# Four kinds of subtraction and addition in the projection sweeps move from GpSimd to VectorE

## The chip, the cores and the metric

The kernel runs on one core of a Trainium2 chip. The metric is the device time of one execution in microseconds. Three executions of the kernel before took 2745.77, 2746.82 and 2751.03 us; the median is 2746.82 us. TensorE (PE) multiplies matrices; VectorE (DVE), ScalarE (ACT) and GpSimd (POOL) do elementwise work; SyncE (SP) issues most transfers. Each engine works through its own list of instructions in a fixed order and waits on semaphores for the others.

## The reference

One layer of a hybrid decoder, for a prompt of 2048 tokens and 64 new tokens (8 sequences of 8), with model width 1024:

```python
xn   = rmsnorm(x, g_pre_mix)
proj = xn @ w_in                      # q_a k_a v_a | q_b k_b v_b r_b | a_lr
o_a  = attn_fn(q_a, k_a, v_a)         # three dilated windows, 8 heads x 64
logf = log_sigmoid(a_lr @ w_a2 + b_a) / 16
o_b, s_new = gla_recurrent(q_b, k_b, v_b, logf, s_gla)   # 4 heads, dk 64, dv 128
o_b  = rmsnorm(o_b, g_gla_norm) * silu(r_b)
x    = x + rmsnorm(concat(o_a, o_b) @ w_o, g_post_mix)
f    = conv_ffn(rmsnorm(x, g_pre_ffn), ...)              # width 2816, gelu
x    = x + rmsnorm(f, g_post_ffn)
```

Everything is float32. `gla_recurrent` takes a running sum of `logf` within each chunk of tokens and exponentials of it; `rmsnorm` needs the sum of squares of each token over 1024 features.

## The kernel before, in words

A float32 product is made of three products in PE's faster float32 format (fp32r). Each operand is split into a high part (`hi`, a rounded copy, made on ACT) and a low part (`lo = src - hi`, one subtraction of two SBUF tensors), and PE sums `hi*hi + hi*lo + lo*hi`. `split` (L67 to L73) does this; its fourth argument names the engine of the low part, "p" for GpSimd and "v" for VectorE. L70 in the profile is the high part, L73 the low part on either engine.

The layer is computed in three stages. The **sweeps** (`sweeps`, from L257) project the normalized input, 512 tokens (576 with the new ones) at a time. The token blocks are numbered c = 0 to 3 and are passed over twice. Sweep B (c = 0, 1, 2, 3, the first 430 us or so) makes the columns of the linear attention (GLA), and the GLA recurrence itself is interleaved with it. Sweep A (c = 3, 0, 1, 2, to about 770 us) makes q, k and v of the window attention, and the attention of the new tokens is interleaved with it. Then come the window attention of the prompt and the tail (output projection and feed-forward network), which runs to the end.

What the change touches, all of it in the sweeps:

- `norm_pre` (L159) sums the squares of the next block's input over the 8 feature tiles: ACT squares a tile into `sq` (one buffer), and an addition collects it in `ssq` (L177). For c = 0 the addition stands on VectorE, for c = 1 to 3 on GpSimd.
- `xhat` (L205) scales the 8 tiles of the next block (L228, two SBUF tensors, on VectorE) and splits them into `xh` and `xl` (L238). The low parts of even tiles stand on VectorE, those of odd tiles on GpSimd. The first block of sweep B has a path of its own (L235).
- `wfill` (L373) loads the weights ahead of their use, a buffer of 512 KB at a time, and splits them into `wh` and `wl`, four buffers of each. Sweep B's 12 weights (numbers 12 and up) are split once, on VectorE, and kept in memory for later blocks; sweep A's 12 are split anew for each of the 4 blocks, with the low part on GpSimd, 48 in all.
- `gla_decay` (L609) makes the running sum of the decay for the two halves of the heads: `lfm` and `gB` on VectorE (L631, L632), an exponential and a logarithm on ACT (L633, L637), a subtraction (L640: GpSimd for c = 1 to 3), and the running sum as a scan on VectorE (L641).

Behind the scan, `gla_p` makes the decayed keys and queries (`gkh` L751, `gqt` L754 and L757, `gqh` L762, `ktb` L768), PE transposes `gkh` into `pkt` (L752), and the state of the recurrence `gS` is updated on VectorE from the PSUM tile `pgo` (copies at L837, updates at L839). The projections of sweep B end in PSUM tiles `pq` and `pv` (three banks in turn, named g1); for the gate columns ACT takes a tanh `th` of `pv` (L695) and VectorE multiplies it with `pv` (L696), which frees the bank. In sweep A VectorE copies `pv` to `vs` (L65) and makes `ql` from `pq` (L432, L73).

The order of the instructions on each engine is not the order of the code: the program is built with `schedule_with_timeline_sim=True`, and a scheduler that has its own estimate of each instruction's time decides where each one stands in its engine's list. An instruction that changes its engine therefore also moves others, on all engines.

## Time and profile before

| | before |
|---|---|
| median of three executions | 2746.82 us |
| the profiled execution | 2747.31 us |
| span of its trace, first to last instruction | 2745.3 us |
| PE busy | 2655.9 us (97%) |
| VectorE busy | 1791.5 us (65%) |
| ScalarE busy | 1270.2 us (46%) |
| GpSimd busy | 587.2 us (21%) |
| mean clock granted to PE | 0.989 |

The trace holds one execution. A row of the timeline gives the start of an instruction in us, its duration, the engine, the source line, the operation, output and inputs, shapes, a count where rows are merged, and in brackets the engine's idle time before it with what ended it. A row of a group of instructions gives the count, then busy us and mean ns of one, then the idle time before them. A row of a table of windows gives, for each stretch, its length, the busy time of PE, PE's weight loads (PEld), DVE, ACT and POOL with their instruction counts, the share of PE's clock that was granted (PEclk), the share of the transfer engines and GB/s. The time outside the span of the profiled execution is 2747.31 - 2745.3 = 2.0 us.

### The profile page before, as it was taken

The numbers are of one execution on the slowest core, as the hardware profiler recorded it, in microseconds if no ns is written. First come the engines' busy times: TensorE is split into PE (matmuls) and PEld (weight loads), VectorE is DVE, ScalarE is ACT, GpSimd is POOL, SyncE is SP. The second block draws the span as 40 slices with busy tenths as digits, with TensorE's granted clock in tenths as the row PEclk, the third lists the DMA queues.
The fourth block names the chain that finished last, engine by engine and source line by source line (L and its number), as shares of the span: only waits on it lengthen the run. The fifth ranks groups of instructions, "written<-read, shape, count | busy, mean of one in ns | idle before, by whom it ended". The sixth has DMA issues, their size and how long they took to land. (4 is left out here: it accounts for less than half of the span.)

```text
span 2745.3 us, 58213 instructions
## 1 busy us (share of the span) xinstructions
PE 2655.9 (97%) x22203; PEld 2520.9 (92%) x22203; DVE 1791.5 (65%) x4338; ACT 1270.2 (46%) x2961; POOL 587.2 (21%) x643
## 2 busy tenths in 40 slices
PE   8999999999999998998999998999999999999997
PEld 6899899888788887998999998999999999999997
DVE  7545544444357776468899889865676665766666
ACT  6535433333368784445555455433344332443332
POOL 4435243433345674012000020000110000200001
PEclk9999999999999999999999999999999999999998
DMA  8755436799776663376677588986698766976654
GB/s 316 254 182 190 165 116 218 264 334 370 267 260 193 191 168 108 127 249 258 249 274 288 196 323 299 341 303 207 239 341 289 279 227 211 327 249 216 215 192 148
DMA packets 287015, 661.67 MB, mean 241 GB/s; under 512 B 32960, under 2 KB 82752, under 8 KB 284688
## 3 DMA queue, kind: packets, MB, share of 16 engines
q1 hardware_dynamic: 256528, 579.53, 61.1%
q0 software_dynamic: 13216, 46.56, 5.1%
q10 hardware_dynamic: 16992, 31.86, 3.1%
q8 instruction: 175, 2.87, 0.4%
q14 instruction: 104, 0.85, 0.1%
HBM read 511.45 MB, written 146.37 MB: 240 GB/s over the span
## 5 line engine op out<-in xcount | busy, mean ns | idle before, releaser
L70 ACT ACTIVATE ws<-wr 128x512 fp32r<-128x512 f32 (+1 forms) x482 | 292.8, 616 | 426.2 <-PE pfe L1628 138.6
L92 PE MATMUL pfd<-hh,ws 128*128 128x264 f32 x2816 | 474.6, 285 | 6.8 <-ACT ws L70 5.6
L92 PEld LDWEIGHTS pfd<-hh,ws 128*128 128x128 f32 x2816 | 400.0, 189 | 9.2 <-ACT ws L70 7.4
L73 DVE TENSOR_TENSOR ws<-wr,ws 128x512 fp32r<-128x512 f32 (+1 forms) x482 | 319.4, 668 | 119.5 <-ACT ws L70 115.7
L92 PE MATMUL pfd<-hl,ws 128*128 128x264 f32 x1408 | 301.5, 285 | 1.8 <-DVE hl L73 1.8
L1628 PE MATMUL pfe<-xh,ws 128*128 128x264 f32 x1496 | 290.3, 286 | 12.1 <-DVE u L1615 7.6
L1628 PE MATMUL pfa<-xh,ws 128*128 128x264 f32 x1496 | 289.8, 285 | 4.5 <-ACT ws L70 1.9
L1628 PE MATMUL pfd<-xh,ws 128*128 128x264 f32 x1408 | 289.3, 285 | 2.1 <-ACT ws L70 1.0
L1628 PEld LDWEIGHTS pfe<-xh,ws 128*128 128x128 f32 x1496 | 236.5, 189 | 13.8 <-DVE u L1615 8.4
L1628 PEld LDWEIGHTS pfa<-xh,ws 128*128 128x128 f32 x1496 | 234.9, 188 | 6.0 <-ACT p L1617 2.4
L399 PE MATMUL pv<-wh,xh 128*128 128x256 f32 (+1 forms) x816 | 236.1, 289 | 1.8 <-DVE th L696 1.8
L1628 PEld LDWEIGHTS pfd<-xh,ws 128*128 128x128 f32 x1408 | 231.3, 189 | 3.1 <-ACT ws L70 1.2
L399 PE MATMUL pv<-wh,xl 128*128 128x256 f32 (+1 forms) x816 | 232.2, 285 | 0.0
L399 PE MATMUL pv<-wl,xh 128*128 128x256 f32 (+1 forms) x816 | 232.2, 285 | 0.0
L92 PEld LDWEIGHTS pfd<-hl,ws 128*128 128x128 f32 x1408 | 225.1, 189 | 2.1 <-DVE hl L73 2.0
L1577 POOL DMA_DIRECT2D xl<-d_xst x52 | 28.1, 541 | 830.8 <-PE pfe L1628 495.4
L1869 ACT ACTIVATE ass<-ass,aml 128x256 f32<-128x256 f32 (+1 forms) x384 | 173.5, 454 | 63.7 <-DVE aml L1865 37.9
L1628 PE MATMUL pfd<-xl,ws 128*128 128x264 f32 x704 | 200.6, 285 | 0.7 <-DMA xl<-d_xst 0.7
L92 PE MATMUL pq<-xh,wh 128*128 128x512 f32 (+2 forms) x480 | 170.9, 364 | 10.7 <-ACT xh L234 7.9
L1628 PE MATMUL pfe<-xl,ws 128*128 128x264 f32 x616 | 175.7, 285 | 0.0
L1628 PE MATMUL pfa<-xl,ws 128*128 128x264 f32 x616 | 174.8, 284 | 0.0
L92 PE MATMUL pq<-xl,wh 128*128 128x512 f32 (+2 forms) x480 | 174.0, 364 | 0.0
(335 smaller groups left out, 6531.6 us busy)
## 6 DMA issues: line engine op xcount, KB each, us to landing
ws<-d_wst SPq DMA_DIRECT2D x248, 512.0 KB, 5.2
wr<-in_wu SPq DMA_DIRECT2D x114, 512.0 KB, 5.0
d_wst<-ws SPq DMA_DIRECT2D x88, 512.0 KB, 4.1
wr<-in_wd SPq DMA_DIRECT2D x160, 256.0 KB, 3.8
wr<-in_wt SPq DMA_DIRECT2D x60, 512.0 KB, 7.0
wh<-d_wbs SPq DMA_DIRECT2D x35, 512.0 KB, 5.6
wl<-d_wbs SPq DMA_DIRECT2D x35, 512.0 KB, 5.8
skp<-in_ckt SPq DMA_DIRECT2D x16, 1024.0 KB, 8.1
```

Source lines behind the costliest of these rows:

```text
L70: h = nc.scalar.activation(hi, src, AF.Copy)
L73: return h, (nc.gpsimd if lo_eng == "p" else nc.vector).tensor_tensor(lo, src, hi.bitcast(F32), op=ALU.subtract)
L92: mm = nc.tensor.matmul(o, ww[:, k, :], xx[:, s0:s0 + n], start=(k == order[0] and i == 0), stop=(k == order[-1] and i == 2))
L399: mm = nc.tensor.matmul(ps[:m, :256], x[:, t0:t0 + m], w[:, k % 4, :], start=(k == 0 and i == 0), stop=(k == KT - 1 and i == 2))
L1577: self.nc.gpsimd.dma_start(t.bitcast(F32), xo[i, z])
L1628: self.lastmm = nc.tensor.matmul(bank[:, :H], w[:, ww, k, :], xx, start=new and k == 0 and j == 0, stop=k == 3 and j == 2, skip_group_chec ...
L1869: ex = nc.scalar.activation(ssb[:, sc:sc + nk], ssb[:, sc:sc + nk], AF.Exp, bias=self.ml[:, idx, h:h + 1], scale=-1.0, accum_out=self.ml[: ...
```

## The change

Four conditions that chose GpSimd are taken out, and VectorE does the work in every case. GpSimd keeps the other GLA multiplications (L701, L757, L762, L768) and the small power functions (L107).

```diff
@@ norm_pre
                 nc.scalar.activation(sq[:, :w], r[:, :w], AF.Square)
-                (nc.gpsimd if c else nc.vector).tensor_tensor(ssq[:, :w], ssq[:, :w], sq[:, :w], op=ALU.add)
+                nc.vector.tensor_tensor(ssq[:, :w], ssq[:, :w], sq[:, :w], op=ALU.add)
@@ xhat
             else:
-                self.split(hi[:, :w], lo[:, :w], r[:, :w], "p" if k % 2 else "v")
+                self.split(hi[:, :w], lo[:, :w], r[:, :w], "v")
@@ wfill
-                w = self.weight(self.a["wt"][i].rearrange("p (k c) -> p k c", k=nk), sh, "v" if i >= 12 else "p")
+                w = self.weight(self.a["wt"][i].rearrange("p (k c) -> p k c", k=nk), sh, "v")
@@ gla_decay
         for i, (m, B) in enumerate(zip(ms, self.gB)):
-            (nc.gpsimd if c else nc.vector).tensor_tensor(m[:, :w], m[:, :w], B[:, :w], op=ALU.subtract)
+            nc.vector.tensor_tensor(m[:, :w], m[:, :w], B[:, :w], op=ALU.subtract)
```

103 instructions leave GpSimd's list and join VectorE's: 48 `wl`, 28 `xl`, 21 `ssq` and 6 `lfm`. The scheduler then sets all lists anew. Three places matter below.

**PE in sweep B, block c = 0**, around the first transpose of the decayed keys (`pkt` from `gkh`). The numbers tell the buffers apart: `pv_603` is the fourth projection block of 128 tokens, `pv_658` the fifth, each of 24 matmuls. Before:

```order
L399 MATMUL pv_603<-wh_404,xl_198 128x256
L399 MATMUL pv_603<-wh_404,xh_206 128x256
L399 MATMUL pv_603<-wl_405,xh_206 128x256
L752 MATMUL pkt_560<-c_ident,gkh_561 128x128
L399 MATMUL pv_603<-wh_404,xl_207 128x256
L399 MATMUL pv_603<-wh_404,xh_210 128x256
```

After:

```order
L399 MATMUL pv_658<-wh_455,xl_198 128x256
L399 MATMUL pv_658<-wh_455,xh_206 128x256
L752 MATMUL pkt_560<-c_ident,gkh_561 128x128
L399 MATMUL pv_658<-wl_456,xh_206 128x256
L399 MATMUL pv_658<-wh_455,xl_207 128x256
L399 MATMUL pv_658<-wh_455,xh_210 128x256
```

The transpose now stands 23 matmuls later in PE's list.

**VectorE at the start of sweep B's block c = 1**, where the decay's scan and the state's copies stand (`gB_1361` and `lfm_1362` are the first half of the heads, `gB_1368` and `lfm_1369` the second). Before:

```order
L641 SCALAR_TENSOR_TENSOR gB_1361<-smask,lfm_1362 128x512
L646 TENSOR_SCALAR gbt_1378<-gB_1361 128x4x4
L647 TENSOR_SCALAR gbt_1378<-gB_1361 128x4
L754 TENSOR_TENSOR gqt_1776<-gB_1361 128x128
L768 TENSOR_TENSOR ktb_128<-ktb_128,gk_1421 128x32
L837 COPY gS_117<-pgo_1479 64x128 x2
L751 TENSOR_TENSOR gkh_1772<-gkh_1772,gk_1421 128x128
L768 TENSOR_TENSOR ktb_128<-ktb_128,gk_1421 128x96
L641 SCALAR_TENSOR_TENSOR gB_1368<-smask,lfm_1369 128x512
L839 SCALAR_TENSOR_TENSOR gS_115<-gS_117,gEc_557,pgo_1506 64x128 x2
```

After:

```order
L640 TENSOR_TENSOR lfm_1362<-lfm_1362,gB_1361 128x512
L641 SCALAR_TENSOR_TENSOR gB_1361<-smask,lfm_1362 128x512
L177 TENSOR_TENSOR ssq_1730<-ssq_1730,sq_2103 128x512
L646 TENSOR_SCALAR gbt_1378<-gB_1361 128x4x4
L647 TENSOR_SCALAR gbt_1378<-gB_1361 128x4
L640 TENSOR_TENSOR lfm_1369<-lfm_1369,gB_1368 128x512
L754 TENSOR_TENSOR gqt_1776<-gB_1361 128x128
L837 COPY gS_117<-pgo_1479 64x128 x2
L641 SCALAR_TENSOR_TENSOR gB_1368<-smask,lfm_1369 128x512
L177 TENSOR_TENSOR ssq_1730<-ssq_1730,sq_2108 128x512
L768 TENSOR_TENSOR ktb_128<-ktb_128,gk_1421 128x32
L839 SCALAR_TENSOR_TENSOR gS_115<-gS_117,gEc_557,pgo_1506 64x128 x2
```

The first copy of the state moves ahead of `ktb`; two additions of `ssq`, each of which waits for a square on ACT, now stand in front of `gbt` and of the state's update at L839.

**VectorE where sweep B passes into sweep A** (`wl_4851` and `wl_5158` are the first two weights of sweep A). Before:

```order
L65 COPY vb_4117<-pv_4792 128x256
L65 COPY gkT_4764<-pkt_4723 128x256
L65 COPY vb_4118<-pv_4818 64x256
L65 COPY vb_4114<-pv_4854 128x256
L65 COPY vb_4115<-pv_4892 128x256
```

After:

```order
L65 COPY vb_4117<-pv_4792 128x256
L65 COPY gkT_4764<-pkt_4723 128x256
L73 TENSOR_TENSOR wl_4851<-wr_4848,wh_4850 128x1024
L65 COPY vb_4118<-pv_4818 64x256
L73 TENSOR_TENSOR wl_5158<-wr_5155,wh_5157 128x1024
L65 COPY vb_4114<-pv_4854 128x256
L65 COPY vb_4115<-pv_4892 128x256
```

The low parts of the weights, which wait for `wh` on ACT, now stand between the copies that empty PSUM banks.

## The prediction

> **What bounds the kernel now.** I read the table of windows first, cut at the ends of sweep B, sweep A and the window attention.

> ```profile
> 0.00:430.00 430.00, 403.80 (x3307) 363.23 (x3308) 239.06 (x581) 215.24 (x567) 182.94 (x238) 0.98 0.61 210
> 430.00:770.00 340.00, 339.48 (x2868) 285.27 (x2867) 135.45 (x289) 110.50 (x169) 132.89 (x76) 1.00 0.81 290
> ```

> PE bounds both sweeps. In sweep A it is idle for 0.5 of 340 us: nothing can be won there. In sweep B it is idle for 26.2 of 430 us. The change can pay only through that idle time, so I read next what ended it, in the table of PE's waits up to 760 us (total, times, longest).

> ```profile
> PE pq L92 <- ACT xh L234: 7.9, 1, 7.9
> PE pgo L843 <- DVE gS L839: 5.0, 2, 4.1
> PE pkt L752 <- DVE gkh L751: 2.3, 1, 2.3
> PE pq L92 <- DVE ql L432: 2.3, 1, 2.3
> PE pgo L830 <- DVE gS L837: 1.9, 1, 1.9
> PE pv L399 <- DVE th L696: 1.8, 1, 1.8
> PE pgo L830 <- DVE gS L839: 1.8, 2, 0.9
> ```

> The first row is the wait for the first input at the start; the change does not touch it. The other six add up to 15.1 us, and VectorE ends every one of them. VectorE is both what the change loads and what PE waits for.

> Some of these waits cost more than their own length. The windows just behind three of them:

> ```profile
> 50.30:53.70 3.40, 3.19 (x15) 3.22 (x16) 3.40 (x9) 3.40 (x14) 3.12 (x5) 0.50 0.43 143
> 57.10:60.60 3.50, 3.50 (x19) 3.50 (x18) 3.26 (x10) 2.80 (x7) 3.27 (x6) 0.51 0.50 170
> 323.40:330.20 6.80, 5.84 (x23) 5.48 (x24) 5.07 (x19) 5.37 (x25) 4.08 (x10) 0.50 0.00 1
> ```

> The granted clock is half there. 13.7 us at half clock are worth up to 6.8 us of PE's work. Idle time and half clock together, 15.1 + 6.8 = 21.9 us, are about all that could be won.

> **What VectorE pays now for GpSimd's work.** The timeline of GpSimd (two rows) and VectorE at the start of sweep A:

> ```profile
> 402.33 2.90 POOL L73 TENSOR_TENSOR wl<-wr,wh 128x1024 fp32r<-128x1024 f32 x1
> 405.19 3.86 POOL L73 TENSOR_TENSOR xl<-raw,xh 128x576 fp32r<-128x576 f32 x2
> ```

> ```profile
> 400.39 2.59 DVE L73 TENSOR_TENSOR xl<-raw,xh 128x576 fp32r<-128x576 f32 x1
> 403.76 2.08 DVE L228 SCALAR_TENSOR_TENSOR raw<-raw,c_gvec,rbp 128x576 f32<-128x576 f32 x1
> 405.77 2.00 DVE L73 TENSOR_TENSOR xl<-raw,xh 128x576 fp32r<-128x576 f32 x1
> 407.69 1.91 DVE L228 SCALAR_TENSOR_TENSOR raw<-raw,c_gvec,rbp 128x512 f32<-128x512 f32 x1
> 410.30 0.69 DVE L73 TENSOR_TENSOR xl<-raw,xh 128x512 fp32r<-128x512 f32 x1 [0.70 <-ACT xh L70]
> 410.90 0.75 DVE L228 SCALAR_TENSOR_TENSOR raw<-raw,c_gvec,rbp 128x512 f32<-128x512 f32 x1
> ```

> The same scaling takes 1.91 us beside GpSimd's `xl` and 0.75 us without it. While GpSimd runs one of its long two-input operations, a two-input operation of VectorE stands still. So the moved work leaves one engine and also ends part of another's delay.

> **The load.** Prices per instruction, from the groups up to 770 us (the fifth from the groups behind it, where GpSimd is nearly idle):

> ```profile
> L73 POOL TENSOR_TENSOR wl<-wr,wh 128x1024 fp32r<-128x1024 f32 x48 | 119.5, 2496 | 156.6 <-ACT wh L70 135.2 <-DMA out_o_vp<-vs 14.1 <-PE pgo L942 6.9
> L73 DVE TENSOR_TENSOR wl<-wr,wh 128x1024 fp32r<-128x1024 f32 x12 | 15.1, 1257 | 3.0 <-ACT wh L70 3.0
> L70 ACT ACTIVATE wh<-wr 128x1024 fp32r<-128x1024 f32 x60 | 63.4, 1056 | 104.6 <-PE pq L92 45.4 <-PE pv L399 28.6 <-issue 14.1
> L177 DVE TENSOR_TENSOR ssq<-ssq,sq 128x512 f32<-128x512 f32 x7 | 4.8, 687 | 0.1
> L73 DVE TENSOR_TENSOR ws<-wr,ws 128x512 fp32r<-128x512 f32 x450 | 306.3, 686 | 109.9 <-ACT ws L70 106.1 <-DMA wr<-in_wu 1.1 <-DMA out_o_y<-acc 0.2
> L73 DVE TENSOR_TENSOR xl<-raw,xh 128x512 fp32r<-128x512 f32 x20 | 24.3, 1220 | 3.1 <-ACT xh L70 3.0
> ```

> VectorE gets 48 x 1.257 = 60.3 us of `wl`; 28 `xl`, 21 `ssq` and 6 `lfm` at 0.69 us each (those of 576 columns by 576/512 more) make another 39 us. That is some 99 us on 374.5 us busy in 770 us. It gets back part of the delays: the 20 `xl` it already makes take 1220 ns where 686 are needed, 10.7 us in that group alone. VectorE would be busy for about 60% of the sweeps. It does not become the bound by its sum; what counts is the places where PE waits.

> **Place A, sweep B's first block (48 to 61 us).**

> ```profile
> 50.51 0.45 PE L752 MATMUL pkt<-c_ident,gkh 128*128 128x128 f32 x1 [2.30 <-DVE gkh L751]
> 50.41 1.40 ACT L767 ACTIVATE ktb<-gB,gbt 128x128 f32<-128x128 f32 x5
> 53.20 1.29 POOL L177 TENSOR_TENSOR ssq<-ssq,sq 128x512 f32<-128x512 f32 x1
> 53.27 2.29 DVE L754 TENSOR_TENSOR gqt<-gB 128x128 f32<-128x128 f32 x3
> 55.95 0.39 PE L399 MATMUL pv<-wh,xh 128*128 128x256 f32 x1 [1.81 <-DVE th L696]
> 46.80 0.28 PE L399 MATMUL pv<-wh,xh 128*128 128x256 f32 x1
> 46.91 0.28 PE L399 MATMUL pv<-wl,xh 128*128 128x256 f32 x1
> ```

> By the new order the transpose stands 23 matmuls later, 23 x 0.11 = 2.5 us: that covers the 2.30 us unless `gkh` is later than now. ACT's new list has one `sq`, one `th` and a table load in front of `gkh`, so I expect about 1 us of lateness, no more. The `th` that PE waits for at 55.95 stood behind three `gqt`, held up by the addition on GpSimd; it now stands ahead of them. The next `th` then sets the pace: ACT has ten of the small exponentials, at 1.40/5 = 0.28 us each, between `gkh` at about 51 us and that `th`, which with VectorE's part comes to about 54.4 us. PE starts the sixth block there, where now it starts the fifth at 55.95, one block of 24 x 0.11 = 2.6 us less far. 55.95 + 2.6 - 54.4 = 4.2 us, and 0.3 for the half clock behind it that goes: **-4.5 us**, between 0 (the wait only moves) and -7.5 (4.1 of waits and 3.4 of half clock).

> [...]

> **Place B, the start of block c = 1 (120 to 140 us).**

> ```profile
> 123.28 1.28 ACT L760 ACT_TABLE_LOAD   x1
> 125.12 0.33 DVE L768 TENSOR_TENSOR ktb<-ktb,gk 128x32 f32<-128x32 f32 x1 [2.19 <-ACT ktb L767]
> 126.04 0.48 PE L830 MATMUL pgo<-vb,gkT 128*128 128x256 f32 x1 [1.86 <-DVE gS L837]
> ```

> VectorE stood idle for 2.19 us here: ACT set the time, through table loads, not GpSimd. The copy of the state now stands ahead of `ktb`, but behind an `ssq` and the second `lfm`, both of which wait for ACT. By the list it can start at about 124.6 instead of 125.38: **-0.8 us**, between +3 (the added `ssq` hold it) and -2.8 (its share of the six rows). Block c = 2 has two waits of 0.9 us behind the same kind of work, with less of ACT in them: **-0.8**, between 0 and -1.8.

> **Place C, block c = 3.**

> ```profile
> 315.12 2.80 POOL L640 TENSOR_TENSOR lfm<-lfm,gB 128x576 f32<-128x576 f32 x2 [11.05 <-ACT gB L637]
> 316.57 2.43 DVE L641 TENSOR_TENSOR_SCAN gB<-smask,lfm 128x512 f32<-128x512 f32 x1 [3.50 <-POOL lfm L640]
> 319.44 1.21 DVE L641 TENSOR_TENSOR_SCAN gB<-smask,lfm 128x512 f32<-128x512 f32 x1
> 324.36 0.79 PE L843 MATMUL pgo<-gS,gqh 128*128 128x256 f32 x1 [4.12 <-DVE gS L839]
> ```

> The scan beside the second `lfm` takes 2.43 instead of 1.21 us: 1.2 us come back. The two `lfm` at 0.75 on VectorE end the wait for GpSimd 1.4 us sooner and then fill the same 1.5 us. In front of the second state update nothing else goes. The wait shrinks to about 2.9 us, and a little of the 3.4 us that the half clock costs: **-1.5**, between +1 and -7.5.

> **Place D, into sweep A (413 us).** PE waited 2.3 us for `ql`, behind the stretched rows shown above. The four stretched rows from 400 us on lost 5.5 us against 0.77 us for 576 columns and 0.69 to 0.75 for 512; two `wl` (2.5 us) and three `xl` (2.3 us) take their place: 5.5 - 4.8, **-0.7**, between +2 and -2.3.

> **Sweep A.** A `wl` on VectorE waits for `wh`, and `wh` for a buffer that PE gives back; behind it in VectorE's list stand the copies that empty PE's banks. On GpSimd 135.2 us of such waiting harmed nobody. The cover is the banks: three in turn, so a copy may be 2 x 2.6 us late before PE stops. A `wh` and its `wl` (1.06 + 1.26 us) fit into that. I put **+0.5 us**, between 0 and +8 (48 of them at 0.17).

> **The sum**: -4.5 - 0.8 - 0.8 - 1.5 - 0.7 + 0.5 = -7.8 us. The profiled execution took 2747.3 us (span 2745.3 and 2.0 around it), so 2739.5; it lies 0.5 above the median shown, so 2739.0.

> **Rivals.**
> - *Only the contention goes, and it was not on the path* (within 0.2%). ACT's one list with its table loads sets places A and B, as the 2.19 us row says. Then only C and D give anything, 2.2 us: 2744.6. Against it: at 55.95 and 316.57 GpSimd's own rows stretch VectorE's.
> - *All of PE's waits go, half clock with them.* 2746.8 - 21.9 = 2725. For it: the stretch is in most of these places. Against: the change adds instructions to the same list.
> - *VectorE's list becomes the wait* (slower). At the starts of the blocks c = 1 to 3 the seven `ssq` each wait for a square on ACT, and `gbt`, scan and state stand behind them. If each of three blocks lost 4 us (seven additions at 0.69 less what was idle) and the half clock followed for 3.4 us each (1.7 lost), it is 3 x 5.7 = +17, less the 5.2 us of A and D: 2759. It decides from 5.2/3 = 1.7 us a block on. For it: rows at 125.12 and 126.04 show the state held up by a neighbour that waits for ACT. Against: VectorE is idle for 191 of 430 us in sweep B.
> - *The weights' low parts hold the banks in sweep A* (slower): 48 x 0.35 us = +17, less the 8.3 us of the other terms: 2755. The 0.5 us of idle time in that sweep now speaks against.

> [...]

> **How the numbers follow.** Forecast 0.50; waits all gone 0.12; not on the path 0.22; VectorE's list 0.11; sweep A's banks 0.05. The range for 8 in 10 is 2727 to 2751: from near the second rival to half of the way to the slower ones; the forecast's own is 2731 to 2741, from twice the sum to the bound of 0.2%. A measurement of this kernel tells 0.2% (5.5 us) from no change. Faster 0.50 + 0.12 = 0.62, same 0.22, slower 0.16.

> **What would show it.** Right: no GpSimd `wl`, `xl` or `ssq`; the scaling at L228 and `xl` near 0.75 and 0.69 us everywhere in the sweeps; PE's waits before 430 us down from 15.1 to 7 to 10 us; the transpose at about 51 us without the half clock; sweep A still without idle PE. Wrong: a wait of more than 4 us at a block's start with `ssq` in front of what PE waits for, or PE idle in sweep A behind `wl`. If the time moves while PE's waits up to 770 us do not, the cause is in the stages behind, which I hold unchanged.

## The result and the profile after

The change makes the kernel faster by about 0.4%.

| | before | after |
|---|---|---|
| median of 20 executions, us | 2747.06 | 2737.48 |
| lowest and highest, us | 2740.91, 2755.08 | 2732.78, 2744.36 |
| ratio, 95% interval | | 0.9964, 0.9955 to 0.9972 |
| span of the profiled execution, us | 2745.3 | 2737.9 |

The medians are 9.6 us apart; 7.8 us were forecast. One execution of one kernel differs from the next by several us, so a place of the program that differs by 1 us between two traces proves nothing by itself.

The table of windows of the kernel after, cut as before:

```profile
0.00:430.00 430.00, 411.90 (x3345) 366.63 (x3346) 262.96 (x643) 218.27 (x578) 104.59 (x188) 1.00 0.61 214
430.00:770.00 340.00, 338.73 (x2868) 284.44 (x2866) 173.52 (x363) 114.11 (x181) 17.32 (x30) 1.00 0.81 292
```

PE is idle for 18.1 us of the first 430, where it was 26.2. In sweep A it is idle for 1.3 of 340 us. VectorE is busy for 436.5 us up to 770, 62 us more than before, although some 99 us of work went to it: the stretching ended. These are its groups up to 770 us:

```profile
L73 DVE TENSOR_TENSOR wl<-wr,wh 128x1024 fp32r<-128x1024 f32 x60 | 73.5, 1225 | 44.7 <-ACT wh L70 37.0 <-DMA raw<-in_xp 6.5 <-ACT qh L431 1.1
L73 DVE TENSOR_TENSOR xl<-raw,xh 128x512 fp32r<-128x512 f32 x40 | 26.8, 684 | 8.3 <-ACT xh L70 8.2
L228 DVE SCALAR_TENSOR_TENSOR raw<-raw,c_gvec,rbp 128x512 f32<-128x512 f32 x24 | 17.7, 751 | 4.9 <-DMA raw<-in_xp 4.5 <-ACT rbp L212 0.3
L641 DVE TENSOR_TENSOR_SCAN gB<-smask,lfm 128x512 f32<-128x512 f32 x8 | 9.8, 1221 | 0.1
```

`xl` took 1220 ns and takes 684; the scaling at L228 took 1104 ns and takes 751. The rows that VectorE ends in the table of PE's waits up to 760 us (total, times, longest; a row of 0.4 us is left out):

```profile
PE pgo L830 <- DVE gS L839: 3.6, 3, 1.9
PE pv L399 <- DVE th L696: 2.2, 3, 1.0
PE pgo L846 <- DVE gS L837: 1.2, 1, 1.2
PE pkt L752 <- DVE gkh L751: 1.1, 2, 0.6
PE pgo L843 <- DVE gS L839: 0.5, 2, 0.3
PE pq L92 <- DVE ql L432: 0.4, 1, 0.4
```

These six rows add up to 9.0 us, where the prediction's six made 15.1; not all name the same pair. With the small rows that both lists leave out it is 9.4 us after 17.5. The half clock in the sweeps was 13.7 us and is 3.4 us, at another place:

```profile
220.62:224.04 3.42, 1.56 (x9) 1.22 (x9) 3.37 (x12) 3.41 (x11) 0.55 (x2) 1.00 0.40 111
224.04:227.45 3.41, 3.41 (x18) 3.41 (x17) 2.43 (x6) 3.41 (x14) 1.80 (x5) 0.50 0.21 39
319.00:330.00 11.00, 10.60 (x74) 9.75 (x74) 9.52 (x36) 10.77 (x46) 6.17 (x14) 1.00 0.27 96
```

The last row is the start of block c = 3: before, PE waited 4.12 us there and ran 6.8 us at half clock; now it is idle for 0.4 of 11 us at the full clock.

### Where the time went, place by place

The projections are the same 3888 matmuls in every kernel of this study, in the same order but for neighbours that change places (119 of them in the kernel after). So the start of the n-th of them can be compared between two traces, and the change of that difference over a stretch is what the stretch won or lost. The table is worked out in this way from the profiled executions. Its columns are the predicted places; the first 44 us, which differ by up to 2.5 us from one execution to the next, are left out. PE's other matmuls lie between the projections and can cross the bound of a column. "Measured" is the difference of the medians from the same session's kernel before.

| kernel (profiled) | A, to 90 us | c = 1, to 184 | c = 2, to 277 | c = 3, to 394 | D, to 446 | sweep A | sum | measured |
|---|---|---|---|---|---|---|---|---|
| *predicted* | -4.5 | -0.8 | -0.8 | -1.5 | -0.7 | +0.5 | -7.8 | |
| the change | -2.5 | +1.2 | +3.8 | -6.7 | -2.9 | -0.8 | -7.9 | -9.6 |
| `wl` alone | -0.3 | -1.5 | +1.1 | -1.0 | -2.8 | +2.4 | -2.1 | -0.5 |
| `xl` alone | +1.1 | -0.6 | +4.6 | -2.6 | 0.0 | -2.2 | +0.3 | +1.3 |
| `ssq` alone | -3.0 | +3.8 | +1.2 | -0.8 | +0.7 | 0.0 | +1.9 | +2.9 |
| `lfm` alone | +1.0 | +2.2 | +1.7 | -5.0 | +0.6 | 0.0 | +0.4 | +1.9 |
| `xl` and `wl` | -0.1 | -0.5 | +4.5 | -5.9 | -2.8 | -0.8 | -5.7 | -7.0 |
| all but `ssq` | -1.3 | +0.2 | +3.8 | -5.8 | -2.8 | -0.8 | -6.6 | -8.7 |
| new lists, old engines | -1.7 | +2.4 | +4.0 | -5.3 | -1.8 | -0.8 | -3.1 | -4.9 |
| old lists, new engines | +0.9 | -1.8 | +1.6 | -5.1 | -2.2 | -0.7 | -7.3 | -9.0 |
| one input on GpSimd | -2.6 | +0.2 | +0.4 | -3.6 | -0.9 | -0.8 | -7.3 | -4.5 |
| squares late, block 3 | -2.5 | 0.0 | +2.4 | -5.6 | -2.9 | -0.8 | -9.3 | -9.7 |
| squares late, blocks 2, 3 | -3.0 | -0.5 | +2.6 | -7.0 | -2.9 | -0.8 | -11.4 | -11.3 |

The sums of the traces lie within 3 us of the measured differences. The total of the forecast holds, but hardly one of its terms does. In these columns the change takes 8.6 us from PE's idle time and 10.2 us from its time at half clock, which is worth 5.1 (in the kernel before, the 128x256 matmuls of L399 start 0.21 us apart at half clock and 0.11 at the full one). That makes 13.7 us, and only 7.9 arrive. Most of the rest goes into PE's own list, as "The loss at c = 2" shows.

### The profile page after: what moved, and what is told of

Same layout as the page of the kernel before. It is cut to its first block, busy times and chain, and to the rows that moved or that the text cites. A ratio compares the mean times of both kernels' runs of the same rounds, so it can differ in the third digit from the quotient of the medians.

```text
span 2737.9 us, 58183 instructions
## 1 busy us (share of the span) xinstructions
PE 2658.4 (97%) x22203; PEld 2518.3 (92%) x22203; DVE 1845.9 (67%) x4441; ACT 1271.2 (46%) x2961; POOL 386.4 (14%) x540
## 5 line engine op out<-in xcount | busy, mean ns | idle before, releaser
L70 ACT ACTIVATE ws<-wr 128x512 fp32r<-128x512 f32 (+1 forms) x482 | 292.9, 616 | 426.8 <-PE pfe L1628 133.6
L92 PE MATMUL pfd<-hh,ws 128*128 128x264 f32 x2816 | 476.7, 286 | 6.0 <-ACT ws L70 4.5
L92 PEld LDWEIGHTS pfd<-hh,ws 128*128 128x128 f32 x2816 | 402.1, 190 | 8.6 <-ACT ws L70 6.4
L73 DVE TENSOR_TENSOR ws<-wr,ws 128x512 fp32r<-128x512 f32 (+1 forms) x482 | 319.2, 668 | 123.7 <-ACT ws L70 118.9
L92 PE MATMUL pfd<-hl,ws 128*128 128x264 f32 x1408 | 303.1, 286 | 1.9 <-DVE hl L73 1.9
L1628 PE MATMUL pfe<-xh,ws 128*128 128x264 f32 x1496 | 291.4, 287 | 11.4 <-DVE u L1615 6.9
L399 PE MATMUL pv<-wh,xh 128*128 128x256 f32 (+1 forms) x816 | 233.9, 287 | 2.2 <-DVE th L696 2.2
L399 PE MATMUL pv<-wl,xh 128*128 128x256 f32 (+1 forms) x816 | 232.1, 284 | 0.0
L399 PE MATMUL pv<-wh,xl 128*128 128x256 f32 (+1 forms) x816 | 232.0, 284 | 0.0
L92 PEld LDWEIGHTS pfd<-hl,ws 128*128 128x128 f32 x1408 | 226.6, 190 | 2.2 <-DVE hl L73 2.1
L92 PE MATMUL pq<-xh,wh 128*128 128x512 f32 (+2 forms) x480 | 173.0, 366 | 8.3 <-ACT xh L234 7.9
L1656 DVE TENSOR_TENSOR acc<-acc,pfd 128x264 f32<-128x264 f32 x304 | 116.3, 422 | 89.6 <-PE pfd L92 89.1
L92 PE MATMUL pq<-xh,wl 128*128 128x512 f32 (+2 forms) x480 | 173.0, 361 | 0.0
```

The source lines that it names most:

```text
L70: h = nc.scalar.activation(hi, src, AF.Copy)
L73: return h, (nc.gpsimd if lo_eng == "p" else nc.vector).tensor_tensor(lo, src, hi.bitcast(F32), op=ALU.subtract)
L92: mm = nc.tensor.matmul(o, ww[:, k, :], xx[:, s0:s0 + n], start=(k == order[0] and i == 0), stop=(k == order[-1] and i == 2))
L399: mm = nc.tensor.matmul(ps[:m, :256], x[:, t0:t0 + m], w[:, k % 4, :], start=(k == 0 and i == 0), stop=(k == KT - 1 and i == 2))
L1628: self.lastmm = nc.tensor.matmul(bank[:, :H], w[:, ww, k, :], xx, start=new and k == 0 and j == 0, stop=k == 3 and j == 2, skip_group_chec ...
L1656: nc.vector.tensor_tensor(acc[m][:, s0:s0 + n], acc[m][:, s0:s0 + n], pz, op=ALU.add)
```

## The experiments

The theory was that GpSimd holds up VectorE where PE waits, and that the gain is this delay with the half clock behind it. The main rival was that the gain comes from the new order of the lists, which any change of engine brings about.

### Each part alone

```diff
# e1_only_wl, against the kernel before
-                w = self.weight(..., sh, "v" if i >= 12 else "p")
+                w = self.weight(..., sh, "v")
# e2_only_xl
-                self.split(hi[:, :w], lo[:, :w], r[:, :w], "p" if k % 2 else "v")
+                self.split(hi[:, :w], lo[:, :w], r[:, :w], "v")
# e3_only_ssq
-                (nc.gpsimd if c else nc.vector).tensor_tensor(ssq[:, :w], ssq[:, :w], sq[:, :w], op=ALU.add)
+                nc.vector.tensor_tensor(ssq[:, :w], ssq[:, :w], sq[:, :w], op=ALU.add)
# e4_only_lfm
-            (nc.gpsimd if c else nc.vector).tensor_tensor(m[:, :w], m[:, :w], B[:, :w], op=ALU.subtract)
+            nc.vector.tensor_tensor(m[:, :w], m[:, :w], B[:, :w], op=ALU.subtract)
```

> Only the low parts of sweep A's 48 weights move to VectorE; ssq, odd xl and lfm stay on GpSimd. My theory (the gain is GpSimd's delay of VectorE at the places where PE waits): only the passage into sweep A has both, so PE's wait of 2.27 us for ql near 413 us shrinks by 1.5 to 2.5 us, sweep A keeps PE busy throughout (less than 2 us idle in 340), nothing before 395 us changes by more than 1 us: 2744.5, that is -1.5 to -3 against before. Rival (the weights' low parts hold the banks in sweep A): PE idle in sweep A grows by 3 us or more, slower than before by 2 or more. Rival (it is the scheduler's new order and not GpSimd): places before 395 us, where no instruction of this kind stands, move by several us either way.

> Only the low parts of the odd input tiles (28) move. My theory: VectorE's scaling (L228) and even xl near the ends of sweep B's blocks go to 0.75 and 0.69 us; PE waits little there, so sweep B wins 1 to 2 us, mostly in the passage into sweep A: 2745, -1 to -3 against before. The waits near 50 to 56 us and 324 us stay (nothing that causes them is touched). Order alone: one of these two waits goes or a new one over 2 us comes.

> Only the 21 additions of squares move. My theory, after the traces of before and after: the place at 48 to 61 us wins 2 to 4 us (the addition no longer stretches gqt), and the start of block c = 2 (205 to 230 us) loses 3 to 5 us, because an ACT square that waits for its input tile stands ahead of the exponential of gB: 2747, within 2 us of before. The start of block c = 3 (324 us) stays. If the loss at block c = 2 is not there, it belongs to lfm or to the combination of parts.

> Only the 6 decay subtractions move. My theory: the start of block c = 3 (315 to 330 us) carries it: the scan is not stretched (1.2 us instead of 2.4) and the two lfm end 1 to 2 us sooner; with the half clock behind the wait 1.5 to 6 us: 2743, -2 to -6 against before. The places at 50 to 56 us and at 413 us stay. If the wait of 4.1 us at 324 us does not shrink, that part of the whole change's gain comes from the order or from the other parts. Sum of the four parts by my theory: about -9, the whole change gave -9.6; by the rival of the order the parts do not add up.

Measured against 2745.15 us in that session: `wl` 2744.63 (ratio 1.000, 0.999 to 1.001), `xl` 2746.46 (1.0004, 0.9994 to 1.0015), `ssq` 2748.06 (1.0019, 1.0008 to 1.0030), `lfm` 2747.03 (1.0005, 0.9996 to 1.0013). No part alone makes the kernel faster, and `ssq` makes it slower. The four differences add up to +5.6 us, the whole change gives -9.6.

The places answer better than the times. At D `wl` alone does nearly all of it (-2.8 of -2.9), but `xl` alone also brings PE's wait for `ql` from 2.27 to 0.8 us; its column shows 0.0 because 16 of PE's other matmuls have moved into it from sweep A. A came with `ssq` (-3.0). At c = 3 it is `lfm` that takes most away. But every part alone also pays, somewhere in blocks 1 and 2, for a new order. For `ssq` that is one wait, in PE's and VectorE's timelines of that kernel:

```profile
129.83 0.79 PE L830 MATMUL pgo<-vb,gkT 128*128 128x256 f32 x1 [5.50 <-DVE gS L839]
```

```profile
121.71 0.58 DVE L837 COPY gS<-pgo 64x128 f32<-64x128 f32 x2
125.12 0.33 DVE L768 TENSOR_TENSOR ktb<-ktb,gk 128x32 f32<-128x32 f32 x1 [2.83 <-ACT ktb L767]
125.38 1.21 DVE L641 TENSOR_TENSOR_SCAN gB<-smask,lfm 128x512 f32<-128x512 f32 x1
```

The second scan stands behind a `ktb` that waits 2.83 us for ScalarE, and the update of the state behind the scan. No `ssq` stands between the copy and that scan. This agrees with the rival of the order, and it left the question open what the engines do with the order held fast.

### The order held fast

To take order and engine apart, the kernel is traced twice: once as the variant whose order is wanted, and once as the variant whose engines are wanted, with every list held to the first one's order (the code is abridged).

```diff
+    VE = {...}                      # parts on VectorE for the order
+    build(nc, arrays)
+    ORDER = [i.name for bb in nc.cur_f.blocks for i in bb.instructions]
+    nc = _bacc.Bacc("TRN2", target_bir_lowering=False, num_devices=1)
+    VE = {...}                      # parts on VectorE for the work
     build(nc, arrays)
...
+        if ORDER:                   # at the end of the trace
+            for i in sorted(instructions, key=place in ORDER):
+                if engine of i in last:
+                    tc.add_manual_dep(i, last[engine], NoSync)
+                last[engine] = i.name
```

> The kernel is traced twice: the first time as the changed kernel, only to take the scheduler's order of all instructions, the second time with the 103 instructions back on GpSimd and every engine's list held to that order. PE, ScalarE and the transfers have the changed kernel's lists; VectorE's lacks the 103, GpSimd's has them in the same order. Theory that the work's engine matters (GpSimd delays VectorE where PE waits): the gain goes: the waits for th near 56 us, for gS near 324 us and for ql near 413 us are back (2, 3 and 2 us or more), 2743 to 2749. Rival that the scheduler's new order alone makes the gain: 2736 to 2740, the waits as short as in the changed kernel.

> The other corner: all lists in the order of the kernel before, the 103 instructions on VectorE, where the order of before puts them. Theory of the engine: 2738 to 2743, gqt near 53 us and the scan near 316 us unstretched, the ql wait near 413 us under 1 us; the wait of the transpose for gkh near 50 us stays (its place in PE's list is the old one). Rival of the order: 2745 or more, since the old order keeps its waits and VectorE has more in front of them.

| median against the session's 2748.0 us | work on GpSimd | work on VectorE |
|---|---|---|
| lists of before | 2748.0 | 2739.03 (0.9969, 0.9957 to 0.9981) |
| lists of the change | 2743.14 (0.9985, 0.9976 to 0.9994) | -9.6 (0.9964, 0.9955 to 0.9972), another session |

The engine alone gives 9.0 us with the old lists. The order alone gives 4.9 us. On top of the engine the order adds 0.6 us, less than can be told apart; on top of the new order the engine adds 4.7 us. So the work's engine carries the gain, and the rival is half right: the order is worth something, but in part the same microseconds, and it takes others back. By the table, the change and the old lists with the new engines differ by -3.4 us at A, -1.6 at c = 3 and -0.7 at D, and by +3.0 at c = 1 and +2.2 at c = 2. c = 3 shows why engine and order don't add up. The scan of the kernel with the new lists and the old engines is still stretched, and the one with the old lists and the new engines isn't (VectorE's timelines, first the former):

```profile
319.85 2.43 DVE L641 TENSOR_TENSOR_SCAN gB<-smask,lfm 128x512 f32<-128x512 f32 x1 [4.89 <-POOL lfm L640]
```

```profile
317.39 1.23 DVE L641 TENSOR_TENSOR_SCAN gB<-smask,lfm 128x512 f32<-128x512 f32 x1
```

and yet both win some 5 us there, since either brings the wait of 4.12 us down to 1.64 and 0.41 or to 1.32 and 0.90 us, and with that the half clock of 6.8 us is gone.

At A the order is what counts. With the old lists and the new engines A gains nothing: the transpose waits 2.30 us where it always did, and the next `th` still comes late, because the addition that was on GpSimd now stands itself between the `gqt` (VectorE's timeline):

```profile
55.02 0.94 DVE L177 TENSOR_TENSOR ssq<-ssq,sq 128x512 f32<-128x512 f32 x1
55.88 0.88 DVE L754 TENSOR_TENSOR gqt<-gB 128x128 f32<-128x128 f32 x2
56.69 0.74 DVE L696 SCALAR_TENSOR_TENSOR th<-th,pv 128x256 f32<-128x256 f32 x2
```

### The change without `ssq`, and `xl` with `wl`

```diff
# e7_without_ssq, against the kernel after
-                nc.vector.tensor_tensor(ssq[:, :w], ssq[:, :w], sq[:, :w], op=ALU.add)
+                (nc.gpsimd if c else nc.vector).tensor_tensor(ssq[:, :w], ssq[:, :w], sq[:, :w], op=ALU.add)
# e8_xl_and_wl: the kernel before with the diffs of e1 and e2
```

> The changed kernel with the additions of squares back on GpSimd. If their place ahead of the decay chain costs the 4 us at the start of block c = 2 (205 to 230 us), that block gains 3 to 4 us and the first block (48 to 61 us) loses the 2.5 us that the additions alone gave: 2736, -1 to -3 against the changed kernel. If the loss at c = 2 belongs to the other parts (xl alone lost 4.6 us there), it stays and the time is 2740 or more.

> Only the two kinds of low parts move together. If the parts add up: the passage into sweep A -2.9 us as for wl alone, block c = 2 up to +4.6 as for xl alone, 2745 to 2747. If VectorE has to be free of GpSimd altogether for the gain (each part alone leaves the other operations to stretch it), more than the sum: 2740 to 2743. The scheduler's rival gives no sign: any value, with places that differ from both single parts.

Without `ssq` the time is 2739.28 us (0.9968, 0.9958 to 0.9978): nothing is lost by leaving the additions on GpSimd, and the loss at c = 2 stays at 3.8 us. So the guess that the additions cause it is refuted. `xl` and `wl` together give 2741.01 us (0.9978, 0.9969 to 0.9986), 7.0 us, where alone they gave 0.5 and -1.3: the low parts carry most of the change, but only together. In the traces the surplus lies at c = 3 (-5.9 against -1.0 and -2.6). The wait there was 3.85 and 3.25 us with one part and is 2.0 with both, and only then does the half clock stay away.

### GpSimd's operations with one input

All lists are held to the order of the kernel before. The operations leave out one of their two inputs, so the results are other numbers than the reference's (the code is abridged):

```diff
-        (nc.gpsimd ...).tensor_tensor(lo, src, hi, op=ALU.subtract)
+        nc.gpsimd.tensor_scalar(lo, hi, 0.000244140625, None, op0=ALU.mult)
-        nc.gpsimd.tensor_tensor(ssq[:, :w], ssq[:, :w], sq[:, :w], op=ALU.add)
+        nc.gpsimd.tensor_scalar(ssq[:, :w], sq[:, :w], 8.0, None, op0=ALU.mult)
-        nc.gpsimd.tensor_tensor(m[:, :w], m[:, :w], B[:, :w], op=ALU.subtract)
+        nc.gpsimd.tensor_scalar(m[:, :w], B[:, :w], -1.0, None, op0=ALU.mult)
```

> Lists, engines and waits of the kernel before, but each of the 103 GpSimd operations has one input tensor instead of two (a multiplication of the high part, of the square or of the logarithm by a constant; so the low parts, sums of squares and decays are other numbers than the reference's). Nothing moves to VectorE. If what costs is that a two-input operation of GpSimd holds up VectorE, VectorE's rows go to 0.69 to 0.75 us for 512 columns, the scan near 316 us to 1.2 us, the waits near 324 and 413 us shrink, and the time is 2737 to 2741, as with the old lists and the new engine. If what costs is that GpSimd is slow and far (its result comes later), VectorE's rows may be short but the waits for gS and th stay: 2744 to 2748. If GpSimd holds up VectorE with one input as well, rows and time stay as before: 2746 to 2749.

2741.22 us against 2745.74 (0.9984, 0.9972 to 0.9995): 4.5 us, where the move to VectorE with the same lists gives 9.0. The two intervals overlap, and in the table both traces win the same 7.3 us, so the sizes are not told apart. The groups up to 770 us (the file's lines are a few further down: L74 is the low part on VectorE, L232 the scaling):

```profile
L73 POOL TENSOR_SCALAR wl<-wh 128x1024 fp32r<-128x1024 f32 x48 | 136.5, 2844 | 151.0 <-ACT wh L70 134.3 <-PE pgo L949 6.9 <-PE pgt L818 3.9
L232 DVE SCALAR_TENSOR_TENSOR raw<-raw,c_gvec,rbp 128x512 f32<-128x512 f32 x24 | 19.8, 843 | 19.3 <-DMA raw<-in_xp 16.5 <-ACT rbp L216 2.7
L74 DVE TENSOR_TENSOR xl<-raw,xh 128x512 fp32r<-128x512 f32 x20 | 14.9, 747 | 3.4 <-ACT xh L70 3.3
```

GpSimd is busy for longer than before (2844 ns for a `wl`, not 2496), and yet VectorE's `xl` takes 747 ns, not 1220. Of the 20 `xl`, 16 run for more than half of their time beside such an operation and take 762 ns on average, 1272 at most. So it is not GpSimd's work as such that holds VectorE up but, in the main, the two-input form of it, and the end of that delay by itself gives about 4.5 us. Whether the work must leave GpSimd for more is not shown by the times. At c = 3 its results still come late: a scan of VectorE waits 2.64 us for GpSimd's `lfm`, and PE waits 2.62 us for the state behind it (PE's timeline, L850 is the matmul at L843):

```profile
320.00 0.48 PE L850 MATMUL pgo<-gS,gqh 128*128 128x256 f32 x1 [2.62 <-DVE gS L846]
```

### The loss at c = 2

In the kernel after, ScalarE's list has a square ahead of the decay's exponential (ScalarE's timeline, then VectorE's, then PE's):

```profile
211.96 0.69 ACT L176 ACTIVATE sq<-raw 128x576 f32<-128x576 f32 x1 [3.26 <-DMA raw<-in_xn]
212.55 0.71 ACT L633 ACTIVATE gB<-gB,c_nba 128x512 f32<-128x512 f32 x1
```

```profile
222.56 0.68 DVE L839 SCALAR_TENSOR_TENSOR gS<-gS,gEc,pgo 64x128 f32<-64x128 f32 x2
```

```profile
223.29 0.70 PE L830 MATMUL pgo<-vb,gkT 128*128 128x256 f32 x2 [1.86 <-DVE gS L839]
```

The square waits 3.26 us for its tile, everything behind it comes late, PE waits 1.86 us and runs at half clock from 224.04 to 227.45 us. One more edge for the scheduler keeps the squares behind the decay (abridged):

```diff
         for t in self.gB:
-            nc.scalar.activation(t[:, :w], t[:, :w], AF.Ln, bias=1.0)
+            self.ln = c, nc.scalar.activation(t[:, :w], t[:, :w], AF.Ln, bias=1.0)
...
-                nc.scalar.activation(sq[:, :w], r[:, :w], AF.Square)
+                s = nc.scalar.activation(sq[:, :w], r[:, :w], AF.Square)
+                if c in (3,) and self.ln[0] == c - 1:      # (2, 3) in e11
+                    self.after(s, self.ln[1])
```

> The changed kernel, with one edge for the scheduler more: the squares of block 3's input (norm_pre) may stand in ScalarE's list only behind the last logarithm of block 2's decay. If the 3.8 us lost at the start of block c = 2 come from the square that waits 3.26 us for its input tile ahead of the exponential of gB, the loss goes: 205 to 230 us back to the level of before, no half clock at 224 us, 2733 to 2735, -2.5 to -4.5 against the changed kernel. If the loss belongs to the table loads or to VectorE's own list, it stays and the time is 2737 or more. Everything before 200 us stays as in the changed kernel.

> The same edge for blocks 2 and 3. The start of block c = 1 (120 to 140 us) lost 1.2 us in the changed kernel, while old lists with the new engine won 1.8 there. If squares in front of the decay chain are the reason there too, another 1 to 3 us: 2731 to 2734. If that block's loss has another reason: as with block 3 alone, 2733 to 2735.

For block 3 alone 2736.05 us (0.9967, 0.9956 to 0.9977), for both 2734.40 us (0.9964, 0.9952 to 0.9976). The half clock at c = 2 is gone in both, and both traces run through the sweeps without any. But c = 2 wins only 1.2 to 1.4 of the 3.8 us; with block 3 alone c = 3 gives 1.1 back. By the ratios neither is told apart from the change as it is.

The rest is not idle time. Waits of 1.27 and 0.99 us stay at c = 2 in both, but the kernel before has two of 0.89 us there, and PE's idle time in that column is only 0.5 us above the kernel before. The rest stands in PE's own list, which the change has altered too. The small projection `plr` (L247), from which the decay is made, has eight matmuls of 512 columns in each of the blocks c = 1 and c = 2. At c = 2 they stand together in the kernel before, and in three pieces in the kernel after (PE's timelines, first the former):

```profile
199.20 1.29 PE L247 MATMUL plr<-raw,g_walr 128*32 128x512 f32 x8
```

```profile
197.99 1.05 PE L247 MATMUL plr<-raw,g_walr 128*32 128x512 f32 x2
198.96 0.66 PE L789 MATMUL pgT<-c_ident,attm 128*128 128x128 f32 x4
199.55 1.05 PE L247 MATMUL plr<-raw,g_walr 128*32 128x512 f32 x4
200.53 0.50 PE L92 MATMUL pq<-xh,wh 128*128 128x512 f32 x1
200.87 0.40 PE L92 MATMUL pq<-xl,wh 128*128 128x512 f32 x1
201.19 1.05 PE L247 MATMUL plr<-raw,g_walr 128*32 128x512 f32 x2
```

A piece of two or of four takes 1.05 us, all eight together 1.29. Seven kernels have this order: the change, `xl` alone, `xl` with `wl`, all but `ssq`, new lists with old engines, and the two with late squares. Over the 30 projections around `plr` all seven lose 1.81 us at c = 1 and 2.04 or 2.05 at c = 2, with the work on VectorE or on GpSimd. The six others differ from the kernel before by -0.5 to +0.9 us there. So about half of the loss at c = 2, and all of that at c = 1, goes with the order of PE's list. No run keeps the eight together with the rest of the new lists as they are, so what they would give back is not measured.

### Filling a wait

The half clock follows PE's idle time in all traces: all 21 windows of 3.41 us at full clock that held 1.95 us or more of it had half clock behind them. To see whether idle time causes it, the kernel before got seven matmuls in front of the one that waits 4.12 us at c = 3, with all lists held (abridged):

```diff
+            if c == 2 and blk == 0:       # the state's block c = 2 is worked off while c = 3 is projected
+                for _ in range(7):
+                    nc.tensor.matmul(po[:, 0:2, :], khT[:, :128], v[:, :256], start=True, stop=True)
             for i in range(2):
                 if not first:
                     self.gate("o", nc.tensor.matmul(po[:, 2 * i:2 * i + 2, :], qh[i], self.Sg[i][old], ...
```

> The kernel before with all lists held to their order, and seven matmuls more (128x256 in f32, operands that are long there, result overwritten) in PE's list just in front of the one that waits 4.12 us for gS near 324 us. Each takes 0.43 us like its neighbours at L830, 3.0 us together: the wait stays as long, but PE is idle for only about 1.1 us of it. If the half clock behind a wait comes from PE's idle share in the window of the clock ahead of it (in the traces so far every window of 3.41 us at full clock with 1.98 us or more of idle time was followed by half clock, none with 1.70 us or less), the half clock of 6.8 us near 324 us goes and the block's start gains 3.0 to 3.4 us with no wait any shorter: 2743 to 2745. If the half clock has another reason, nothing is gained: 2746 to 2749, half clock near 324 us as before.

2748.66 us against 2745.14 (1.0010, 1.0001 to 1.0020), no gain but a loss. The experiment failed, since the filling waited itself (PE's timeline):

```profile
323.03 5.51 PE L843 MATMUL pgo<-vb,gkT 128*128 128x256 f32 x14 [4.23 <-DVE gS L839]
```

It writes into the tile `pgo`, which VectorE's update of the state reads, so it may start only behind that update. It shows what extra work in the wrong place costs, and nothing about the clock. So no run here changes the idle time alone, and that it causes the half clock, rather than only going with it, is not shown.

## Why the prediction was right, and where it wasn't

The forecast of 2739.0 us (2727 to 2751) met 2737.5. Point by point:

- **"VectorE ends every one of the six waits", and PE bounds the sweeps.** Right for the waits: six rows of 15.1 us became six of 9.0, inside the forecast 7 to 10, and sweep A stayed almost without idle PE (1.3 us in 340). "The change can pay only through that idle time" left out that a new list also changes how long PE itself works.
- **"While GpSimd runs one of its long two-input operations, a two-input operation of VectorE stands still."** Right: 28 operations of VectorE that started beside one in the kernel before ended 0.54 to 0.62 us behind it, and with the work moved L228 and `xl` went from 1104 and 1220 ns to 751 and 684. With one-input operations on GpSimd the delay of `xl` all but ended, with GpSimd busier than before. The engine alone, with the order held, makes 9.0 us.
- **Place A, -4.5.** It was -2.5. The step that failed is "PE starts the sixth block there", at 54.4 us. The transpose did move without harm and the half clock went, but PE's sixth block began at 56.93 (PE's timeline after):

```profile
53.64 0.30 PE L752 MATMUL pkt<-c_ident,gkh 128*128 128x128 f32 x1 [0.50 <-DVE gkh L751]
56.93 0.38 PE L399 MATMUL pv<-wh,xh 128*128 128x256 f32 x1 [0.99 <-DVE th L696]
```

  It had to wait for the `th` of 56.47, which still had three `gqt` ahead of it (VectorE's timeline):

```profile
55.33 1.22 DVE L754 TENSOR_TENSOR gqt<-gB 128x128 f32<-128x128 f32 x3
56.47 0.41 DVE L696 SCALAR_TENSOR_TENSOR th<-th,pv 128x256 f32<-128x256 f32 x1
```

  I had taken the `th` that moved ahead of them and priced the next one by ScalarE alone. And the reason was only half right: with the old lists the same work on VectorE gives nothing here, with the new lists on GpSimd 1.7.
- **Blocks c = 1 and c = 2, -0.8 each.** They lost 1.2 and 3.8 us. The bound of +3 stood for c = 1, none above 0 for c = 2. The step that failed is that the sum has no term for PE's own list: `plr` in three pieces costs 1.8 us at c = 1 and 2.0 at c = 2. PE's idle time at c = 1 did fall, by 1.0 us, near the forecast. At c = 2 it rose by 0.3 us and brought 1.7 us of half clock. I saw VectorE's list at c = 1 and left out that the scheduler makes such a list for each block; a square that waits 3.26 us for a transfer ahead of the exponential was not in any row I had read. That part, about 2 us, is the third rival's kind of mechanism, but not its culprit: with `ssq` back on GpSimd the loss at c = 2 is the same.
- **Place C, -1.5.** It was -6.7, near the bound of -7.5. The failed step is "in front of the second state update nothing else goes". In the new list the update moved up to stand between the two scans, and PE's wait went but for 0.24 us (VectorE's timeline after):

```profile
317.68 1.22 DVE L641 TENSOR_TENSOR_SCAN gB<-smask,lfm 128x512 f32<-128x512 f32 x1
318.99 0.68 DVE L839 SCALAR_TENSOR_TENSOR gS<-gS,gEc,pgo 64x128 f32<-64x128 f32 x2
319.71 1.23 DVE L641 TENSOR_TENSOR_SCAN gB<-smask,lfm 128x512 f32<-128x512 f32 x1
```

  The second failure is "a little of" the half clock: it did not shrink in step with the wait but went by whole windows of 3.4 us (6.8 us behind a wait of 4.12, 3.4 behind 3.85 with `wl` alone, none behind 2.0 with `xl` and `wl`).
- **Place D, -0.7.** It was -2.9. I set the added `wl` and `xl` (4.8 us) against the stretch that ends (5.5 us) as if both stood in front of `ql`. VectorE has room for the added ones: it idles 2.21 us ahead of `ql`, waiting for ScalarE (408.14 us). PE's wait went from 2.27 to 0.43 us. `wl` alone does all of it, and `xl` alone brings the wait to 0.8 us.
- **Sweep A, +0.5.** It was -0.8, within what two executions differ by. PE's idle time was 1.3 of 340 us with all 48 low parts on VectorE. That the three banks cover them was my estimate; no run shows it.
- **The rivals.** "The contention was not on the path" and "the weights' low parts hold the banks" fell. "All waits go, half clock with them" is what happened at c = 3 and at no other place. That the gain is the scheduler's order I hadn't named as a rival; it is worth 4.9 us alone and nothing that can be measured on top of the engine.

So the total was right by luck, because errors of both signs cancelled: A, c = 1 and c = 2 came out 8.6 us worse than forecast, C, D and sweep A 8.7 us better. Less idle time and less half clock gave 13.7 us from 44 us on, nearly twice the forecast, and `plr` in pieces took 4.2 back (0.4 of them at c = 3); what took the other 1.6 us stays open.

## What to carry to other kernels

A small gain under a list scheduler is a sum of places that win and lose several times as much, so a move can be worth nothing in each of its parts and pay as a whole; test it whole, and with the order held when the cause matters. Compare the lists of every engine, that of the bound one first: here small matmuls that stood together were cut apart and took back some 4 us. Long two-input operations on GpSimd were paid for twice here, in its own time (2496 ns for a `wl`, 1257 on VectorE) and in VectorE's two-input operations beside them (1.91 us for a scaling, 0.75 without); look for that first where a queue behind VectorE ends PE's waits. Price a wait of PE with the clock behind it: in these profiles every window of 3.41 us at full clock with 1.95 us or more of idle PE was followed by one at half clock, which cost up to 1.7 us more.

## What the hardware showed

```profile
408.72:412.13 3.41, 2.50 (x19) 2.24 (x17) 2.52 (x5) 1.08 (x2) 2.12 (x3) 1.00 0.84 249
412.13:415.55 3.42, 2.06 (x14) 2.06 (x15) 2.52 (x7) 2.25 (x5) 3.10 (x2) 1.00 0.93 298
415.55:418.96 3.41, 3.41 (x25) 3.30 (x25) 0.50 (x2) 1.43 (x2) 0.77 (x2) 1.00 1.03 393
```

and of the latter, where it lies within one:

```profile
410.50:413.91 3.41, 1.12 (x8) 0.87 (x7) 2.36 (x6) 1.99 (x4) 1.85 (x2) 1.00 0.88 277
413.91:417.32 3.41, 3.41 (x13) 3.41 (x14) 1.89 (x6) 1.19 (x4) 2.51 (x2) 0.50 0.96 349
```

This also fits c = 3. A wait of 4.12 us leaves 1.95 us or more in one window however the grid lies. Counting the wait and half of the half clock behind it, the kernel before pays 4.1 + 3.4 = 7.5 us there, `xl` alone 3.25 + 1.7 = 5.0, `xl` with `wl` 2.0, `lfm` alone 2.16 + 0.39 = 2.55, the change 0.16 + 0.24 = 0.4. The differences from 7.5 (2.6, 5.5, 5.0 and 7.1) are near what the column c = 3 has: 2.6, 5.9, 5.0 and 6.7. It fits `wl` alone less well: 3.85 + 1.7 leaves 2.0, and the column has 1.0. How much of the scatter between executions comes from where the grid lies wasn't measured.

**Which operations of GpSimd hold VectorE up.** With two inputs: in the kernel before, a scaling took 1.91 us beside such an operation and 0.75 without. In its sweeps 28 operations of L228 and `xl` started 0.25 us or more before the end of a two-input operation that GpSimd was running. All of them ended 0.54 to 0.62 us behind that end; with nothing beside them they take 0.68 to 0.82 us in all. With one input it was much less: `xl` took 747 ns on average, where it takes 684 in the kernel after, in a trace where 16 of 20 ran mostly beside GpSimd operations of 1.5 to 2.8 us; the longest took 1272.
